# A transpose of 128 attention weights moves from one PSUM bank group to another in a two-layer hybrid attention block

## The chip, the cores and the metric

The kernel runs on one core of one Trainium2 chip. The metric is device time in microseconds: the median of three runs. One further execution was taken with the hardware profiler; all rows of the profile come from that one.

Engine names in the profile: PE is the matmul engine (PEld its weight loads), DVE the vector engine, ACT the scalar engine, POOL the general one, SP the queue that issues most DMAs. Lines (L933) are lines of the kernel's file.

## The reference

Two layers over a sequence of 512 tokens of width 1024 on float32. Each layer is a half-weighted feed-forward part with a layer norm, a token mixer with a layer norm, and a second feed-forward part with a layer norm:

```python
for l in range(DEPTH):
    x = _layer_norm(DN_ALPHA * x + 0.5 * _swiglu(x, ffn1_w1[l], ffn1_w2[l]), ln1_g[l], ln1_b[l])
    mix = _token_mix(x, w_in[l], ...)
    x = _layer_norm(DN_ALPHA * x + mix, ln2_g[l], ln2_b[l])
    x = _layer_norm(DN_ALPHA * x + 0.5 * _swiglu(x, ffn2_w1[l], ffn2_w2[l]), ln3_g[l], ln3_b[l])
```

The mixer runs three kinds of attention with eight heads of 64 each, gates their outputs and projects the sum:

- *Swa*: a window of 128 keys with a sink in the softmax.
- *Fox*: causal attention over all 512 keys, with a decay summed from forget gates.
- *Nsa*: three softmaxes for each query, each with a gate of its own: over 31 compressed keys (blocks of 32 tokens, stride 16, put through a small network), over selected blocks of 64 keys, and over a window of 512 keys. With 512 tokens there are eight blocks and eight are selected, so the second covers all of them.

The part that the change touches is the first softmax of Nsa, the weights of the compressed keys, `p_c`, on their way to `o_c = p_c @ vc`.

## The kernel before

**Stages.** Each layer is a feed-forward stage, a mixing stage and a second feed-forward stage. A float32 matrix product is made of three matmuls on high and low parts (`mm3`, L163 to L171): every weight chunk of 1024 x 128 is loaded by SP, ACT copies out its high part (`hi`, L148), and DVE subtracts to get the low part (`lo`, L149).

**The mixing stage.** The attention of two heads (index `m`) and one block of 128 queries (index `qb`) is a *unit*: an object of class Swa, Fox or Nsa with three methods. `s` makes the logits on PE (tiles sS, sF, sC, sN), then the softmax on DVE, ACT and POOL. `tr` transposes the weights on PE, 128 x 128 at a time, into PSUM tiles (ptS, ptF, ptN, ptC); `ev_pt` (L510 to L516) copies each tile back over the weights, every second one on DVE (L514) and the others on ACT (L516). `pv` multiplies values by the transposed weights into the tile po (L783, L833, L940, L946).

Units go in batches: eight of Swa, then for each `m` one batch of four (Fox and Nsa of q blocks 0 and 1) and two of two (Fox and Nsa of q block 2, then of 3). `step(cur, prev, n)` (L1115) takes one batch through `s` and the batch before it through `tr`, in slots: parts of `s`, some filler, two tiles of transposes, more filler. Filler (`pump`) is projections: chunks for later units and for the gates, each of eight parts of three matmuls (pj, L169 to L171). At the end of a step come two more filler parts, then all `pv` products of the batch in one po tile, and ACT copies that tile out, one 128 x 128 piece for each unit (L1161).

In a Nsa unit `tr` (L921) works through the two heads: for the first head one ptN tile (two, if the unit has far keys, q blocks 2 and 3), then ptC with the compressed weights of both heads, then the ptN tiles of the second head. So ptC is the second tile of a pair with ptN ahead of it (q block 0 or 1), or the first with ptN behind it.

**PSUM.** It has eight banks, shared out by tag (L77): two for `mm` (filler), three for `sc` (logits), two for `tp` (transposes and a few small tiles), one for `po`. A new tile of a tag waits until a bank of that tag is free, which is when all instructions that read the tile in it are done.

**What sets the order.** `tc.manual_schedule(engines={PE, POOL})` (L87): PE and POOL run in the order in which the code is written. PE does not overtake: if one matmul waits, all behind it wait. For ACT, DVE and SP a planner chooses the order when the program is built, from a timing that it works out itself, by the order in the code; `ev_pt` has a higher priority. Semaphores for all dependencies and for reuse of banks are put in by the framework. Each engine then runs through its own list.

Of the kernel before, what the change touches and what calls it, by code (L numbers as in the profile page):

```python
# [18 lines left out]
P = 128  # L19
# [45 lines left out]
def body(tc, a, out, depth=DEPTH):  # L65
# [15 lines left out]
    def ps(tag=None, name="ps", shape=(P, 512)):  # L81
        if tag is None:
            tag = PS_ALL[ring[0] % 8]
            ring[0] += 1
        return psp.tile(list(shape), F32, name=name, tag=tag, bufs=PS_TAGS[tag])
# [385 lines left out]
    def mix(l, wts, pend, done_ffn, xap, xa, nxt):  # L471
# [37 lines left out]
        def ev_pt(dst, src, n):  # L509

            eng[0] += 1
            with tc.high_priority(100):
                if n and eng[0] % n == 0:
                    nc.vector.tensor_copy(dst, src)  # L514
                else:
                    nc.scalar.activation(dst, src, AF.Copy)  # L516
# [118 lines left out]
        def conv(ws):  # L635
# [52 lines left out]
            def end():  # L688
                while narrow or c.n < 16:
                    feed()  # L690
                    narrow.popleft()()
                tr()
# [39 lines left out]
        class Swa:  # L732
# [37 lines left out]
            def tr(u):  # L770
                pv = u.p.rearrange("p s (b q) -> p s b q", q=P)[:, :, 0:u.nb]
                pt = ps("tp", "ptS", (P, 2, 2, P))[:, :, 0:u.nb]
                for s in range(2):
                    for b in range(u.nb):
                        nc.tensor.transpose(pt[:, s, b], pv[:, s, b], ident)
                ev_pt(pv, pt, 2)
                yield
# [59 lines left out]
        class Nsa:  # L837
# [83 lines left out]
            def tr(u):  # L921
                for s in range(2):
                    for p in u.n[s]:
                        pt = ps("tp", "ptN", (P, 2, 2, P))[:, 0:p.shape[1]]
                        for k in range(p.shape[1]):
                            for br in range(2):
                                nc.tensor.transpose(pt[:, k, br], p[:, k, br], ident)
                        ev_pt(p, pt, 2)
                        yield
                    if s == 0:  # L930
                        pc = u.pc.rearrange("p s n -> p (s n)")
                        pt = ps("tp", "ptC", (P, P))
                        nc.tensor.transpose(pt, pc, ident)  # L933
                        ev_pt(pc, pt, 2)
                        yield
# [134 lines left out]
        chunk(CKV + 4 * P, nsa_k(1))  # L1070
        chunk(CQA, set_q(m.qa, 0))
        fill.insert(len(fill) - 5, tr)
        fill.insert(len(fill) - 2, lambda: conv2(cv))
        fox_chunks(1)
# [291 lines left out]
```

## Time and profile before

| | |
|---|---|
| median of 3 runs | 2500.32 us |
| the runs | 2500.82, 2500.32, 2498.01 us |
| the profiled execution | 2500.47 us |
| its span, first to last instruction | 2498.8 us |
| granted clock of PE | 0.998 |
| instructions in the profile | 40246 |
| ptC transposes on PE (L933) | 32, in the mixing stages |
| their copies | 16 on DVE (mean 288 ns), 16 on ACT (mean 272 ns) |
| po copies on ACT (L1161) | 96 (mean 278 ns) |
| first and last ptC | at 511.9 and 1919.4 us |

How to read it: the span is covered by PE's instructions almost without a gap, and 1.7 us of the execution lie outside the span. In a timeline row stand the start, the time from the first instruction's start to the last one's end, the engine, the line, the operation, the tile written and the tiles read, the shape, how many instructions are merged, and in brackets the idle time of the engine before them with what ended it. Matmuls overlap, so the length of a row on PE is longer than the distance to the next row. In a row of waits stand who waited, for whom, the total in us, how often and the longest.

### The profile page before, as it was taken

The numbers are of one execution on the slowest core, as the hardware profiler recorded it, in microseconds if no ns is written. First come the engines' busy times: TensorE is split into PE (matmuls) and PEld (weight loads), VectorE is DVE, ScalarE is ACT, GpSimd is POOL, SyncE is SP. The second block draws the span as 40 slices with busy tenths as digits, with TensorE's granted clock in tenths as the row PEclk, the third lists the DMA queues.
The fourth block names the chain that finished last, engine by engine and source line by source line (L and its number), as shares of the span: only waits on it lengthen the run. The fifth ranks groups of instructions, "written<-read, shape, count | busy, mean of one in ns | idle before, by whom it ended". The sixth has DMA issues, their size and how long they took to land.

```text
span 2498.8 us, 40246 instructions
## 1 busy us (share of the span) xinstructions
PE 2477.1 (99%) x15547; PEld 2182.7 (87%) x15547; DVE 1655.7 (66%) x3397; ACT 1089.3 (44%) x2131; POOL 234.6 (9%) x454
## 2 busy tenths in 40 slices
PE   9999999999999999999999999999999999999998
PEld 8999887788888889998899998877888888899986
DVE  7888355587654369984479973566776534799834
ACT  4444334576642234443334443345666323344431
POOL 4000000133300000000000000002332000000000
PEclk9999999999999999999999999999999999999999
DMA  7345334633143333334323353445321534234431
GB/s 204 104 126 158 122 100 131 176 80 88 43 143 96 120 114 93 110 119 152 101 95 111 109 166 96 133 122 144 98 77 35 152 101 143 85 94 118 155 108 59
DMA packets 378095, 286.15 MB, mean 115 GB/s; under 512 B 17464, under 2 KB 349384, under 8 KB 377904
## 3 DMA queue, kind: packets, MB, share of 16 engines
q1 hardware_dynamic: 370496, 258.68, 35.5%
q0 software_dynamic: 7408, 24.90, 2.8%
q8 instruction: 122, 2.00, 0.3%
q14 instruction: 69, 0.57, 0.1%
HBM read 256.22 MB, written 17.88 MB: 110 GB/s over the span
## 4 chain that ended last, share of the span: by engine, by line
PE 95%; DVE 2%; DMA 1%; ACT 1%; issue 1%; DVEq 0%; POOLq 0%; ACTq 0%; POOL 0%; SPq 0%
PE pg L363 14%; PE acc L184 8%; PE acc L183 8%; PE acc L182 8%; PE pu L363 7%; PE pj L169 5%; PE pj L170 5%; PE pj L171 5%; PE pv L363 3%; PE gate L169 3%; PE gate L170 3%; PE gate L171 3%; PE brp L170 2%; PE brp L169 2%; PE brp L171 2%; PE sN L885 2%
## 5 line engine op out<-in xcount | busy, mean ns | idle before, releaser
L149 DVE TENSOR_TENSOR lo<-raw,hi 128x1024 fp32r<-128x1024 f32 (+2 forms) x346 | 406.0, 1180 | 484.9 <-ACT hi L148 473.2
L148 ACT ACTIVATE hi<-raw 128x1024 fp32r<-128x1024 f32 (+2 forms) x346 | 351.3, 1024 | 674.2 <-PE acc L183 230.4
L169 PE MATMUL pj<-xh,hi 128*128 128x512 f32 (+1 forms) x720 | 267.1, 371 | 0.2 <-ACT hi L148 0.2
L171 PE MATMUL pj<-xh,lo 128*128 128x512 f32 (+1 forms) x720 | 254.8, 354 | 0.0
L170 PE MATMUL pj<-xl,hi 128*128 128x512 f32 (+1 forms) x720 | 254.6, 354 | 0.0
L182 PE MATMUL acc<-hi,hs 128*128 128x512 f32 x640 | 249.7, 390 | 0.0
L184 PE MATMUL acc<-lo,hs 128*128 128x512 f32 x640 | 249.3, 389 | 0.0
L183 PE MATMUL acc<-hi,hs 128*128 128x512 f32 x640 | 249.2, 389 | 0.0
L363 PE MATMUL pg<-xh,hi 128*128 128x256 f32 x816 | 231.5, 284 | 0.9 <-ACT sn L370 0.9
L363 PE MATMUL pg<-xh,lo 128*128 128x256 f32 x816 | 231.2, 283 | 0.0
L363 PE MATMUL pg<-xl,hi 128*128 128x256 f32 x816 | 231.2, 283 | 0.0
L304 ACT ACTIVATE hi<-ws 128x1024 fp32r<-128x1024 f32 x136 | 142.4, 1056 | 131.4 <-DVE ws L296 76.0
L305 DVE TENSOR_TENSOR lo<-ws,hi 128x1024 fp32r<-128x1024 f32 x136 | 165.0, 1217 | 4.5 <-ACT hi L304 4.4
L363 PEld LDWEIGHTS pg<-xh,hi 128*128 128x128 f32 x816 | 156.8, 192 | 1.8 <-ACT sn L370 1.5
L363 PEld LDWEIGHTS pg<-xl,hi 128*128 128x128 f32 x816 | 156.8, 192 | 0.3
L363 PEld LDWEIGHTS pg<-xh,lo 128*128 128x128 f32 x816 | 156.8, 192 | 0.0
L363 PE MATMUL pu<-tl,hi 128*128 128x256 f32 x544 | 154.1, 283 | 0.0
L363 PE MATMUL pu<-th,lo 128*128 128x256 f32 x544 | 154.1, 283 | 0.0
L363 PE MATMUL pu<-th,hi 128*128 128x256 f32 x544 | 154.1, 283 | 0.0
L171 PEld LDWEIGHTS pj<-xh,lo 128*128 128x128 f32 x720 | 136.3, 189 | 19.6
L169 PEld LDWEIGHTS pj<-xh,hi 128*128 128x128 f32 x720 | 136.7, 190 | 15.4 <-issue 3.1
L170 PEld LDWEIGHTS pj<-xl,hi 128*128 128x128 f32 x720 | 136.9, 190 | 11.5 <-DVE xl L1312 0.2
(324 smaller groups left out, 5951.6 us busy)
## 6 DMA issues: line engine op xcount, KB each, us to landing
raw<-in_ffn_w_dram SPq DMA_DIRECT2D x264, 512.0 KB, 3.9
raw<-in_w_in_dram SPq DMA_DIRECT2D x56, 512.0 KB, 4.0
raw<-in_w_gate_dram SPq DMA_DIRECT2D x48, 512.0 KB, 4.1
x_sp<-xa POOLq DMA_DIRECT2D x24, 512.0 KB, 6.1
ks<-hl SPq DMA_DIRECT2D x96, 128.0 KB, 2.4
xa<-x_sp POOLq DMA_DIRECT2D x16, 512.0 KB, 5.5
raw<-in_w_out_dram SPq DMA_DIRECT2D x16, 512.0 KB, 3.4
tab<-bvec SPq DMA_DIRECT2D x16, 256.0 KB, 3.9
```

Of the source, the lines that this page charges most:

```text
L148: nc.scalar.activation(hi[:, c], raw[:, c], AF.Copy)
L149: nc.vector.tensor_tensor(lo[:, c], raw[:, c], hi[:, c].bitcast(F32), op=OP.subtract)
L169: nc.tensor.matmul(o, hi[:, k], vh, start=first, stop=False)
L170: nc.tensor.matmul(o, hi[:, k], vl, start=False, stop=False)
L171: nc.tensor.matmul(o, lo[:, k], vh, start=False, stop=last)
L182: nc.tensor.matmul(o, sh(k)[:, t], hi[:, c], start=k == 0, stop=False)
L183: nc.tensor.matmul(o, sl(k)[:, t], hi[:, c], start=False, stop=False)
L184: nc.tensor.matmul(o, sh(k)[:, t], lo[:, c], start=False, stop=k == nk - 1)
L304: nc.scalar.activation(hi, x, AF.Copy)
L305: tt(lo, x, hi.bitcast(F32), op=OP.subtract)
L363: nc.tensor.matmul(o, wx, vx, start=first and k == 0 and i == 0, stop=k == 3 and i == 2, skip_group_check=True)
L885: nc.tensor.matmul(o[:, 0:nb].rearrange("p k b j -> p (k b j)"), q, kx[:, 2 * b0:2 * (b0 + nb)].rearrange("p a b -> p (a b)"), start=i == ...
```

## The change

The tile ptC asks for a bank of the tag `po` and no longer of `tp`:

```diff
                     if s == 0:
                         pc = u.pc.rearrange("p s n -> p (s n)")
-                        pt = ps("tp", "ptC", (P, P))
+                        pt = ps("po", "ptC", (P, P))
                         nc.tensor.transpose(pt, pc, ident)
                         ev_pt(pc, pt, 2)
                         yield
```

The tag `po` has one bank. In each step it holds the tile of the value products from the first `pv` matmul to the last copy of L1161; between that copy and the next step's products it is now also taken by ptC, once in a step with q block 2 or 3, and twice, one after the other, in a step with q blocks 0 and 1. The transposes of ptN, ptF and ptS, and the small tiles, stay in `tp`. PE's order, the number of instructions and the arithmetic are the same; the planner makes ACT's, DVE's and SP's lists anew.

## Prediction

> **What bounds the kernel now.** I read first the page's busy times and its chain, then the view of waits for PE alone, then the timeline around each of those waits. On the page I look for the engine that never rests.
>
> ```profile
> PE 2477.1 (99%) x15547; PEld 2182.7 (87%) x15547; DVE 1655.7 (66%) x3397; ACT 1089.3 (44%) x2131; POOL 234.6 (9%) x454
> ...
> PE 95%; DVE 2%; DMA 1%; ACT 1%; issue 1%; DVEq 0%; POOLq 0%; ACTq 0%; POOL 0%; SPq 0%
> ```
>
> PE is busy 99% of the span and carries 95% of the chain that ends last. The kernel is PE's own instruction stream, in an order written out by hand, and the change adds or removes none of it. So only PE's pauses can be won, and only new pauses can be lost. The view of waits for PE has them all (total us, how often, longest):
>
> ```profile
> PE xT L1309 <- DMA xa<-in_x_dram: 4.6, 1, 4.6
> PE ptN L927 <- DVE pc L514: 3.0, 2, 1.5
> PE ptN L927 <- ACT p L516: 1.0, 2, 0.5
> PE ptS L775 <- ACT p L516: 0.9, 2, 0.5
> PE pg L363 <- ACT sn L370: 0.9, 2, 0.6
> PE ptC L933 <- ACT p L516: 0.5, 2, 0.2
> PE pj L169 <- ACT hi L148: 0.2, 1, 0.2
> ```
>
> L514 and L516 are the two forms of ev_pt, the copy of a transposed tile out of PSUM. Three of the rows are transposes of an Nsa unit that wait for such a copy, each twice, once in each of the two layers: 3.0 + 1.0 + 0.5 = 4.5 us. These are waits for one of the two tp banks. The row of ptS belongs to Swa steps, ahead of any ptC in the layer, and the others to stages that the change does not touch.
>
> **The three places.** The idle time in that view counts PE busy until the modelled end of its last matmul, so I take the distance from start to start instead. First number: start; second: length of the group.
>
> ```profile
> 511.25 0.38 PE L927 MATMUL ptN<-ident,p 128*128 128x128 f32 x2
> 511.85 0.30 PE L933 MATMUL ptC<-ident,pc 128*128 128x128 f32 x1 [0.23 <-ACT p L516]
> ...
> 531.21 0.27 PE L933 MATMUL ptC<-ident,pc 128*128 128x128 f32 x1
> 531.32 0.60 PE L927 MATMUL ptN<-ident,p 128*128 128x128 f32 x4
> ...
> 547.12 0.27 PE L933 MATMUL ptC<-ident,pc 128*128 128x128 f32 x1
> 547.89 0.66 PE L927 MATMUL ptN<-ident,p 128*128 128x128 f32 x4 [0.49 <-ACT p L516]
> ...
> 593.34 0.28 PE L933 MATMUL ptC<-ident,pc 128*128 128x128 f32 x1
> 595.10 0.63 PE L927 MATMUL ptN<-ident,p 128*128 128x128 f32 x4 [1.49 <-DVE pc L514]
> ```
>
> At 531.21 nothing is in the way, and the next transpose starts 0.11 us behind ptC. That is the price of one transpose on PE, and it stays, wherever its result goes. Against this measure the places cost:
> - first: two ptN and then ptC, 0.60 us where 0.22 would do: 0.38;
> - second: 547.12 to 547.89 is 0.77, less 0.11: 0.66;
> - third: 593.34 to 595.10 is 1.76, less 0.11: 1.65.
>
> Together 2.69 us in a layer, 5.38 us in both. This is the ceiling of what the change can win here.
>
> **The change part by part.** *Removed:* the 16 ptC of each layer no longer take a tp bank. In all three places ptC is either the waiter or the tile that took the bank which the waiter needed. In the first, ptC itself is held up and would find po empty. In the second and third, the first ptN of the unit had already been copied out by DVE, and ptC then took that bank:
>
> ```profile
> 545.53 0.69 DVE L514 COPY p<-ptN 128x512 f32<-128x512 f32 x1 [0.43 <-PE ptN L927]
> ...
> 592.01 0.69 DVE L514 COPY p<-ptN 128x512 f32<-128x512 f32 x1 [0.29 <-PE ptN L927]
> ```
>
> The first of these copies ends at 546.22, and without the pause the stalled ptN would start at 547.12 + 0.11 = 547.23. The second ends at 592.70, against 593.34 + 0.11 = 593.45. With ptC elsewhere the late ptN takes the bank that these copies emptied 1.0 and 0.75 us before, and has nothing to wait for. No other tile of tp fares worse: taking tiles out of a two-bank sequence puts every remaining tile's predecessor in its bank as early as before, or earlier.
>
> *Moved, at no cost:* the transpose itself and its copy. Which engine copies follows from a counter that goes on counting as before, so DVE and ACT do the same copies of the same sizes.
>
> *Added:* two waits on the single po bank. First, ptC waits until ACT has made the copies of L1161 out of the step before. Second, the step's po products wait until ev_pt has copied ptC. PE works in order, so whatever a wait costs there is paid by every filler matmul behind it. The closest case for the first wait, ACT's list and then PE's:
>
> ```profile
> 555.97 0.45 ACT L1161 ACTIVATE o<-po 128x128 f32<-128x128 f32 x2 [1.32 <-PE po L946]
> ...
> 557.51 1.06 ACT L148 ACTIVATE hi<-raw 128x1024 fp32r<-128x1024 f32 x1 [0.19 <-PE pj L170]
> ```
>
> ```profile
> 557.90 0.38 PE L927 MATMUL ptN<-ident,p 128*128 128x128 f32 x2
> 558.12 0.27 PE L933 MATMUL ptC<-ident,pc 128*128 128x128 f32 x1
> ```
>
> The copies end at 556.42 and ptC starts at 558.12: 1.70 us to spare. This is a step with q blocks 0 and 1, where ptC stands in the second pair of transposes; elsewhere ptC comes later in its step. ACT idles 1.32 us before those copies, waiting for PE: it takes them up at once. The closest case for the second wait, ACT and PE again:
>
> ```profile
> 613.61 0.27 ACT L516 ACTIVATE pc<-ptC 128x128 f32<-128x128 f32 x1
> ```
>
> ```profile
> 615.04 0.44 PE L833 MATMUL po<-p,v 128*64 128x128 f32 x4
> ```
>
> 613.88 to 615.04 leaves 1.16 us. So both new waits cost nothing as the lists of ACT and DVE now stand. No row shows a wait on po by a transpose, so I keep both ends: nothing, since both have over a microsecond to spare, up to the slower rival below. I take nothing, the value to which these rows are nearest.
>
> On these waits a page has a rule against the change. The Trainium skill, "Perfetto Trace Analysis", section Optimizing Tensor Performance, Matmuls, advises that independent matmul groups rotate through different PSUM banks, so that copying one out overlaps the next group; one bank for ptC and the products gives that up. By that rule ptC and the copies of L1161 run one behind the other; by the rows they do so already, 1.70 us apart, and the sum stays. The Trainium skill, "PSUM — Partial Sum Buffer", section PSUM bank collisions raise a hardware error, adds that two engines must keep off one bank even at different columns, so ptC would have to wait for the last of the copies and not only for those it overwrites; 1.70 us is counted from the last one, and the sum stays again.
>
> **What is late next.** PE coming earlier does not make DVE and ACT earlier where these are full. Next come the products of the same step, which read the last transposed tile. ACT and PE, second place; then PE and DVE, third place:
>
> ```profile
> 551.49 0.51 ACT L900 ACTIVATE p<-p,stN 128x256 f32<-128x256 f32 x1 [1.25 <-DVE stN L725]
> ...
> 553.10 0.57 ACT L516 ACTIVATE p<-ptN 128x512 f32<-128x512 f32 x1
> ```
>
> ```profile
> 553.98 1.26 PE L946 MATMUL po<-p,v 128*64 128x128 f32 x20
> ...
> 601.13 1.92 PE L946 MATMUL po<-p,v 128*64 128x128 f32 x32
> ```
>
> ```profile
> 599.15 0.69 DVE L514 COPY p<-ptN 128x512 f32<-128x512 f32 x1
> ...
> 604.20 0.29 DVE L514 COPY p<-ptF 128x128 f32<-128x128 f32 x1 [2.91 <-PE ptF L826]
> ```
>
> - Second place. L946 is the line of the products. By then PE is 0.38 + 0.66 = 1.04 us ahead, and L946 would start at 552.94. The copy that it reads ends at 553.67, and stands behind an ACT that waited for DVE; DVE's timeline has no idle entry between 545.53 and that point, and its start at 545.53 waits for a ptN that only the first place has brought forward, by 0.38. So the copy ends at 553.29, and L946 waits 0.35. Kept so far: 0.69.
> - Third place. PE is 0.69 + 1.65 = 2.34 ahead at 601.13, which makes 598.79. DVE waited for a ptN at 592.01, and its timeline has no idle entry from there to the end of its copy at 599.84, and 0.69 earlier that is 599.15. L946 waits until then: 0.36 lost. Kept: 1.98 us.
> - After that DVE stood idle for 2.91 us, waiting for PE, so it has room to follow, and nothing more is given back.
>
> The sum: 1.98 us in a layer, 3.96 in both. The profiled execution, 2500.47 us, becomes 2496.5; the median of the runs, 2500.32, stands 0.15 us below that execution and becomes **2496.4 us**. As a difference of 0.16% it is less than the 0.2% (5.0 us) which a measurement of this kernel can about tell from no change.
>
> **The rivals.**
> - *Nothing is given back.* ACT's and DVE's orders are not written out: the planner sets them from its own timing of PE's order and the bank waits, and with the wait gone it may put the copies of the last ptN earlier. ACT had 1.25 us of idle time just before 551.49. Then 5.4 us are kept or, with a pause elsewhere gone too, somewhat more: 2494.9. For it speaks that idle time, against it that DVE is full in the third place, whatever the order.
> - *Nothing is won.* The banks were not what PE waited for, or the planner's new order puts other copies late by as much as is won. The named releasers speak against the first: all are copies out of tp. For the second speaks that the order decides by tenths of a microsecond in three places already. Time: 2498 to 2503, say 2500.
> - *Slower: the po wait takes over.* Place: the three steps of each layer with q blocks 0 and 1, after the first in a layer. If the planner puts weight splits (L148, 1.06 us each) ahead of the L1161 copies on ACT, ptC waits and all PE's filler behind it. It decides from the second split on, since 2.12 exceeds 1.70; with three it costs 3.18 - 1.70 = 1.48 us at each of six places, 8.9 in all: 2496.4 + 8.9 = 2505.3. Against it: ACT now reaches the copies idle, with nothing ahead of them.
>
> The rule on rotating banks, in the Trainium skill's "Perfetto Trace Analysis" as above, is this last rival; the trace so far bears out the distance of 1.70 us and no wait.
>
> **How the numbers follow.** My forecast (1.9 to 5 us won) has 0.42; nothing given back, 0.26; nothing won, 0.20; slower by the po wait, 0.12. Faster by over 0.2% is the second case, 0.26; within 0.2% the first and third, 0.62; slower 0.12. The range runs from 2493.5, the ceiling of 5.4 and 1.4 for the scatter of the runs (2498.01 to 2500.82), to 2503, the upper end of the third case; the dear end of the po wait stays outside.
>
> **What would show it.** In the waits of PE after the change, the rows of ptN and ptC behind L514 and L516 are gone. If the give-back is real, po L946 appears there behind ACT and DVE copies, each 0.3 to 0.4 us. Right in the second rival: these rows stay, or new ones of sN, sC or pj stand beside them. Right in the third: ptC waits for ACT o L1161. If PE's waits in the two mixing stages sum to more than now, the prediction is wrong, and the order of ACT's and DVE's lists is the first place to look. A change in the feed-forward stages would be one for which I have no cause.

## The result

| | before | after |
|---|---|---|
| median of 14 runs each | 2500.47 us | 2494.04 us |
| lowest and highest | 2498.01, 2502.91 | 2492.38, 2498.15 |
| the profiled execution | 2500.47 us | 2494.47 us |
| its span | 2498.8 us | 2492.8 us |
| granted clock of PE | 0.998 | 0.998 |

The ratio of the times is 0.9976, with a 95% interval of 0.9968 to 0.9983: faster by 0.24%, 4.3 to 8.0 us. The two profiled executions differ by 6.0 us. This lies a little beyond what the prediction called the ceiling (5.4 us, which the interval still holds), and beyond its forecast (3.96 us, just outside the interval).

The page of the kernel after, busy times and chain, as they were shown of before:

```profile
PE 2476.4 (99%) x15547; PEld 2182.5 (88%) x15547; DVE 1656.1 (66%) x3397; ACT 1089.0 (44%) x2131; POOL 225.1 (9%) x454
...
PE 98%; DVE 1%; DMA 0%; ACT 0%; issue 0%; DVEq 0%; POOLq 0%; SPq 0%; POOL 0%; ACTq 0%
```

PE has as many matmuls as before and as much busy time, in a shorter span. Its share of the chain rose from 95% to 98%. Most of this rise is not the change's: between 50 and 250 us, ahead of the first mixing stage, some 75 us of the chain ran over other engines before and next to none after. The waits of PE after (the whole view: who waited, for whom, total us, how often, longest):

```profile
PE xT L1309 <- DMA xa<-in_x_dram: 4.6, 1, 4.6
PE ptS L775 <- ACT p L516: 0.9, 2, 0.5
```

The rows of ptN and ptC are gone, and no row of po has come. The rows of pg and pj have gone too, in stretches where every engine's order is the same in both kernels, so this is not the change's doing. The two profiles differ there for a reason that stays open: the kernel after left the program's start 1.5 us behind (last section), and PE of the kernel before lost 1.65 us up to 240 us, most of it at pg at 140.6 and 223.2 us. From there on, up to the first mixing stage, the two kernels are within 0.2 us of each other.

The three places in the timeline of PE after (start, length, as before):

```profile
511.16 0.38 PE L927 MATMUL ptN<-ident,p 128*128 128x128 f32 x2
511.38 0.27 PE L933 MATMUL ptC<-ident,pc 128*128 128x128 f32 x1
...
546.60 0.27 PE L933 MATMUL ptC<-ident,pc 128*128 128x128 f32 x1
546.70 0.60 PE L927 MATMUL ptN<-ident,p 128*128 128x128 f32 x4
...
592.08 0.27 PE L933 MATMUL ptC<-ident,pc 128*128 128x128 f32 x1
592.19 0.60 PE L927 MATMUL ptN<-ident,p 128*128 128x128 f32 x4
```

From start to start it is now 0.22, 0.10 and 0.11 us, the price of transposes with nothing in the way; it was 0.60, 0.77 and 1.76. PE's order is the same in both kernels, so each of its 15547 matmuls can be set against its twin. The lead of the kernel after grows at the three places by 0.389, 0.656 and 1.654 us, together 2.70, and in the mixing stages no step takes more than 0.1 us of it back. Over the mixing stage of the first layer it grows by 2.95 us, over that of the second by 2.92, together 5.87. The 0.25 that the three places do not explain come in small steps. The largest is a fourth place of the same kind; here are PE's rows of before, then of after:

```profile
640.84 0.27 PE L933 MATMUL ptC<-ident,pc 128*128 128x128 f32 x1
641.02 0.63 PE L927 MATMUL ptN<-ident,p 128*128 128x128 f32 x4
```

```profile
637.92 0.27 PE L933 MATMUL ptC<-ident,pc 128*128 128x128 f32 x1
638.03 0.60 PE L927 MATMUL ptN<-ident,p 128*128 128x128 f32 x4
```

Before, ptN stood 0.18 us behind ptC, 0.07 more than undisturbed, and another 0.03 was lost inside the ptN group. No idle time is shown there: ptC's modelled end (641.11) lies beyond ptN's start.

**Why nothing was given back.** In the second place the prediction had the last ptN's copy on ACT end late. ACT's rows of after, then PE's:

```profile
550.89 0.57 ACT L516 ACTIVATE p<-ptN 128x512 f32<-128x512 f32 x1
...
552.55 0.31 ACT L867 ACTIVATE pc<-pc,stN 128x32 f32<-128x32 f32 x1
```

```profile
552.74 1.92 PE L946 MATMUL po<-p,v 128*64 128x128 f32 x32
```

The copy ends at 551.46, 1.28 us ahead of the products. In ACT's list of before, both exponentials of L867 stood ahead of this copy; in the new list they come after it and after two more of L900. The second of them and the copy, in the kernel before:

```profile
552.79 0.30 ACT L867 ACTIVATE pc<-pc,stN 128x32 f32<-128x32 f32 x1
...
553.10 0.57 ACT L516 ACTIVATE p<-ptN 128x512 f32<-128x512 f32 x1
```

In the third place the copy is on DVE:

```profile
597.31 0.69 DVE L514 COPY p<-ptN 128x512 f32<-128x512 f32 x1
598.03 0.90 DVE L730 TENSOR_SCALAR p<-p,stN,gt 128x128 f32<-128x128 f32 x2
...
601.27 0.29 DVE L514 COPY p<-ptF 128x128 f32<-128x128 f32 x1 [1.43 <-PE ptF L826]
```

```profile
598.21 1.92 PE L946 MATMUL po<-p,v 128*64 128x128 f32 x32
```

It ends at 598.00, 0.21 us ahead of L946. The two L730 that now follow it stood ahead of it in the list of before:

```profile
596.13 0.61 DVE L730 TENSOR_SCALAR p<-p,stN,gt 128x128 f32<-128x128 f32 x2
...
599.15 0.69 DVE L514 COPY p<-ptN 128x512 f32<-128x512 f32 x1
```

DVE is as full as it was; what changed is which of its work comes first. In the two traces PE, POOL and SP run in the same order; ACT's order differs at 52 of its 2131 positions and DVE's at 106 of 3397, all of them in the mixing stages, between 514 and 1837 us of the kernel before.

**The new waits on po.** The closest case of each in the first layer, ACT's rows of after and then PE's:

```profile
554.73 0.45 ACT L1161 ACTIVATE o<-po 128x128 f32<-128x128 f32 x2 [1.47 <-PE po L946]
...
610.68 0.26 ACT L516 ACTIVATE pc<-ptC 128x128 f32<-128x128 f32 x1
```

```profile
556.88 0.27 PE L933 MATMUL ptC<-ident,pc 128*128 128x128 f32 x1
...
612.12 0.44 PE L833 MATMUL po<-p,v 128*64 128x128 f32 x4
```

From the end of the copies of L1161 (555.18) to ptC are 1.70 us, as predicted; from the end of ptC's copy (610.94) to the products 1.18, against 1.16. In the second layer the same two distances are 1.70 and 1.14 us.

### The profile page after: what moved, and what is told of

Its sections match the earlier page's. It is cut to its first block, busy times and chain, and to the rows that moved or that the text cites. A ratio compares the mean times of both kernels' runs of the same rounds, so it can differ in the third digit from the quotient of the medians.

```text
span 2492.8 us, 40236 instructions
## 1 busy us (share of the span) xinstructions
PE 2476.4 (99%) x15547; PEld 2182.5 (88%) x15547; DVE 1656.1 (66%) x3397; ACT 1089.0 (44%) x2131; POOL 225.1 (9%) x454
## 4 chain that ended last, share of the span: by engine, by line
PE 98%; DVE 1%; DMA 0%; ACT 0%; issue 0%; DVEq 0%; POOLq 0%; SPq 0%; POOL 0%; ACTq 0%
PE pg L363 16%; PE pu L363 8%; PE acc L184 8%; PE acc L182 8%; PE acc L183 8%; PE pj L169 5%; PE pj L170 5%; PE pj L171 5%; PE pv L363 4%; PE gate L169 3%; PE gate L170 3%; PE gate L171 3%; PE brp L171 2%; PE brp L170 2%; PE brp L169 2%; PE sN L885 2%
## 5 line engine op out<-in xcount | busy, mean ns | idle before, releaser
L148 ACT ACTIVATE hi<-raw 128x1024 fp32r<-128x1024 f32 (+2 forms) x346 | 351.3, 1024 | 677.7 <-PE acc L183 230.3
L169 PE MATMUL pj<-xh,hi 128*128 128x512 f32 (+1 forms) x720 | 267.0, 371 | 0.1
L169 PEld LDWEIGHTS pj<-xh,hi 128*128 128x128 f32 x720 | 136.7, 190 | 15.3 <-issue 3.1
```

The source lines that it names most:

```text
L148: nc.scalar.activation(hi[:, c], raw[:, c], AF.Copy)
L169: nc.tensor.matmul(o, hi[:, k], vh, start=first, stop=False)
```

## The experiments

All kernels start from the kernel after, and each ratio is against the kernel before. **Theory A** explains the result so: a transpose waits no more once its tile has a bank that is idle at that moment, and the gain is kept because the planner put the late copies ahead of other work. **Theory B** is the rival, and each expectation says what it means for its run.

**late_copy: the last ptN copy goes back to its old place.** In q block 3 it is held behind the exponentials of L867 on ACT (m = 0) and behind two L730 on DVE (m = 1), as in the lists of before; a second line of the same form keeps two exponentials of L900 in their order, and otherwise the lists are those of the kernel after. `m.pce` and `m.n0` name the exponential and the L730 that it waits behind. The edit's core:

```diff
-                        ev_pt(p, pt, 2)
+                        with tc.issue_after((m.pce, m.n0)[u.m].ins) if u.qb == 3 and s and p is u.n[1][1] and u.m < 2 else tc.high_priority(100): ev_pt(p, pt, 2)
```

> The changed kernel with four copies held back, two in each layer: in the second place (the step before the products of m = 0, q block 3) ACT makes the last ptN copy behind the two exps of L867, as in the kernel before; in the third place (m = 1) DVE makes it behind two norms of L730, as before. Nothing else in any engine's order differs from the changed kernel. Theory A (the lead on PE was kept because the planner's new order puts these copies earlier): po L946 waits in all four places, 0.3 to 0.5 us each, 1.4 to 1.8 us in all; the span goes from 2492.8 to 2494.2 to 2494.6. Theory B (the copies would have been early enough in the old order too, the reckoning of the give-back was wrong in itself): no wait at L946, span 2492.6 to 2493.0.

Median 2496.4 us (11 runs), ratio 0.9987 (0.9978 to 0.9996). ACT and PE at the second place, then DVE and PE at the third:

```profile
550.64 0.31 ACT L867 ACTIVATE pc<-pc,stN 128x32 f32<-128x32 f32 x1
...
550.95 0.57 ACT L516 ACTIVATE p<-ptN 128x512 f32<-128x512 f32 x1
```

```profile
551.05 2.48 PE L946 MATMUL po<-p,v 128*64 128x128 f32 x32
```

```profile
596.21 0.60 DVE L730 TENSOR_SCALAR p<-p,stN,gt 128x128 f32<-128x128 f32 x2
596.84 0.69 DVE L514 COPY p<-ptN 128x512 f32<-128x512 f32 x1
```

```profile
597.11 2.44 PE L946 MATMUL po<-p,v 128*64 128x128 f32 x32
```

Now the copies end 0.47 and 0.42 us after the products' first matmul, and the row of 32 matmuls takes 2.48 and 2.44 us, where it takes 1.92 in the kernel after. Against that kernel's matmuls, PE falls back at L946 by 0.57 and 0.52 us in the first layer and by 0.57 and 0.53 in the second: 2.19 us, more than the 1.4 to 1.8 of theory A. This is the give-back of the prediction, at its two places, and it is there only when the copies stand behind that work as before. The span of the profile, 2493.2 us, fits neither theory's range; this execution left the program's start 1.5 us ahead of the kernel after's (last section), so the two spans cannot be set against each other. The median moves the same way, 2.4 us up, but the intervals of the two ratios overlap; it is the matmuls' starts that decide. PE's view of waits has no row of L946 in this kernel (its only rows are those of xT and ptS, as after): counted from the modelled end of the matmul ahead, 551.43, PE idles 0.14 us before the late matmul at 551.57, too little to show. These waits show only from start to start.

**again: the kernel after, unchanged,** run beside n2_po, c_first and kv_sc below.

> The changed kernel once more, beside the next three on the same chip. Both theories: the same as before, 2492.5 to 2496 us, ratio to the kernel before 0.997 to 0.998; PE's waits hold xT and ptS only.

2493.84 us (9 runs), ratio 0.9976 (0.9967 to 0.9986): the result repeats. PE's waits hold one row that was not expected, pj L169 behind ACT's L148, 0.5 us at the start of the program (8.4 us).

**q3_only: only q block 3's ptC goes to po.**

```diff
-                        pt = ps("po", "ptC", (P, P))
+                        pt = ps("po" if u.qb == 3 else "tp", "ptC", (P, P))
```

> Only the ptC of q block 3 go to po, 8 of 32; the others stay in tp. Theory A (the gain is the sum of single places): the second and third place and the small one at 641 us are gone (0.71, 1.68 and 0.10 us in a layer by the shifts), the first stays (0.42): the span is 0.8 us over the changed kernel's, 2493.6, and PE's waits show ptC behind L516 0.5 us in 2 cases. Theory B (the gain is spread over the step, through the planner's order): the span lies between 2494 and 2498.

One run, 2493.86 us. The wait of the first place is back in PE's waits, and those of the second and third (ptN) stay away:

```profile
PE ptS L775 <- ACT p L516: 0.9, 2, 0.5
PE ptC L933 <- ACT p L516: 0.5, 2, 0.2
```

Against the kernel after, PE falls back by 0.39 us at the first place and by as much at its twin in the second layer, and nowhere else in the mixing stages by more than 0.15 us (at hid, L657, the network of the compressed keys). So the gain is a sum of single places, and ptC of q block 3 alone earns the second and third place. The one run's time says nothing on 0.7 us, nor does its span of 2492.2 us, below both theories': this execution too left the program's start 1.5 us ahead.

**sc_bank: ptC in a bank of the logits (sc) and not in po.** If any bank outside tp would do, this should be as fast.

```diff
-                        pt = ps("po", "ptC", (P, P))
+                        pt = ps("sc", "ptC", (P, P))
```

> The changed kernel with ptC in one of the three sc banks, those of the logits, and not in po. Theory A (what counts is a bank that is idle when ptC comes; po is, the sc banks are not, they turn over with every unit): the waits of ptN behind L514 and L516 are gone as well, but ptC, sF or sN wait for logits and copies in their place; span 2494 to 2500. Theory B (anything out of tp serves): span 2492.5 to 2493.1, and no new row among PE's waits.

2501.16 us (10 runs), ratio 1.0006 (0.9997 to 1.0015): all of the gain is lost. From PE's waits:

```profile
PE ptC L933 <- DVE stN L725: 2.8, 6, 0.6
PE sN L885 <- DVE stF L725: 1.4, 2, 0.7
...
PE sN L885 <- ACT pc L516: 0.9, 2, 0.5
```

The waits of ptN are gone here too, but ptC now waits until DVE has read logits (L725), and logits wait for other logits or until ptC is copied out. It is po's idle time that pays, not the relief of tp alone.

**n2_po: the ptN tiles of the second head go to po as well,** so that ptC and they take turns in one bank.

```diff
-                        pt = ps("tp", "ptN", (P, 2, 2, P))[:, 0:p.shape[1]]
+                        pt = ps("po" if s else "tp", "ptN", (P, 2, 2, P))[:, 0:p.shape[1]]
```

> The changed kernel, and the ptN tiles of the second head go to po too, so that ptC and the ptN behind it take the one bank in turn. Theory A (one bank without rotation makes each transpose wait for the copy of the one before): from the distances of the ptC and their copies in the kernel before, 0.5 to 2.4 us each for twelve pairs in a layer, 11 us, 23 in both, less what later waits absorb; 2508 to 2520 us, with ptN behind L514 and L516 as the largest rows of PE's waits. Theory B (a wait on po is covered by what is queued elsewhere): under 2498.

2527.3 us (4 runs), ratio 1.0109 (1.0095 to 1.0122): slower, and by more than was expected. From PE's waits:

```profile
PE ptN L927 <- ACT pc L516: 13.9, 12, 2.4
PE ptN L927 <- DVE pc L514: 6.7, 12, 1.5
```

At 24 of the 32 ptC, where ptN comes directly behind, it now waits for ptC's copy; at the other eight, filler stands between them. Here the rule of the Trainium skill, "Perfetto Trace Analysis", section Optimizing Tensor Performance, Matmuls, that independent groups should rotate through different banks, holds: 20.6 us of waits at 24 places. From start to start the loss in the mixing stages is 35.9 us: about 27.7 at ptN, 1.8 at the products of Fox and 6.2 in stretches where the clock is halved, which the last section shows. The spans differ by 32.3 us, since this profile's start, without the half clock, was 3.2 us ahead.

**c_first: all ptC at the start of the step,** right behind the copies of L1161, with po as their bank.

```diff
+            for u in prev:
+                if u.br == 0: u.trc()
             it, iu = chain(u.tr() for u in prev), chain(u.s() for u in cur)
```

Here `trc` holds the four lines of ptC, which `tr` no longer has.

> The changed kernel with the ptC transposes of a step moved ahead of everything else in the step, directly behind the products of the step before; the alternation of the copies between ACT and DVE shifts with them. This is the po wait of my slower rival, with the distance of 1.70 us taken away. Theory A (only that distance hides the wait): PE waits for the copies of L1161, about 1.0 us in each of twelve steps of a layer, and the second ptC of four steps for the copy of the first, 0.6 us; 14 us in a layer, 2515 to 2535 us, ptC behind ACT o L1161 in PE's waits. Theory B (PE's queue or other slack covers it): under 2500.

2527.08 us (4 runs), ratio 1.0112 (1.0098 to 1.0126). The time is in the expected range by luck: from PE's waits less than a third of the loss is the one that was meant (its lines are three further down: L936 is ptC, L1164 the copies of po):

```profile
PE ptC L936 <- POOL pc L730: 13.8, 9, 2.7
PE ptC L936 <- ACT o L1164: 7.5, 10, 1.0
...
PE ptC L936 <- POOL p L730: 2.1, 4, 0.6
```

The bank costs 7.5 us at 10 places, up to 1.0 us each, once its distance of 1.70 us is taken away. More, 13.8 us, is that the weights are not ready so early: POOL still scales them. So the run shows that the wait on po exists, and does not show that it alone would cost 33 us.

**kv_po and kv_sc: the row of ptS.** The transposes ptS wait 0.9 us in the two layers together, in `tp`, for the bank which the small tile kv has taken. kv goes to po in the one and to sc in the other:

```diff
-            p = ps("tp", "kv", (P, 3, 64))
+            p = ps("po", "kv", (P, 3, 64))
```

> The changed kernel, and the small tile kv (conv2) goes from a tp bank to po as well. Theory A (a transpose waits on PE because a longer-lived tile holds one of the two tp banks; po is free between the copies of one step and the products of the next): the last wait of a transpose, ptS behind L516, 0.64 us from start to start in each layer, is gone; 1.3 us less, span 2491.5. Theory B (the second bank is not what ptS waits for, or kv keeps po so long that the products wait): the row stays, or po L783 appears among the waits of PE; span 2492.8 or more.

> The changed kernel, and kv goes to a bank of sc. Until the first Fox step those three banks serve one unit at a time, and kv is read out 3.3 us before the next logits come. Theory A (a bank that is idle at that moment is what counts): ptS no longer waits, 0.67 us in a layer, and no products wait for vbd either; the span is 1.3 us below that of the changed kernel beside it, no row but xT among PE's waits. Theory B (the time that ptS saves is waited for again a step later, whichever bank kv is in, since vbd comes late): no difference to the changed kernel.

kv_po: 2493.0 us (10 runs), ratio 0.9975 (0.9965 to 0.9984). The row of ptS is gone, and in PE's waits and timeline stands another:

```profile
PE po L783 <- ACT vbd L713: 1.2, 2, 0.6
```

```profile
494.23 0.88 PE L783 MATMUL po<-p,v 128*64 128x128 f32 x12 [0.60 <-ACT vbd L713]
```

In each layer PE gains 0.70 us at ptS, and loses 0.67 at the next products: the bank is held until ACT has copied kv in L713, and that copy waits for POOL. That the span, 2491.3 us, is near theory A's is chance, since this execution left the program's start 1.5 us ahead of the kernel after's; by the rows theory B is right. kv_sc: 2493.1 us (9 runs), ratio 0.9973 (0.9963 to 0.9983). Its whole view of PE's waits:

```profile
PE xT L1309 <- DMA xa<-in_x_dram: 4.5, 1, 4.5
PE pj L169 <- ACT hi L148: 0.2, 1, 0.2
```

Nothing takes the place of the wait: against again, PE gains 0.70 us at ptS in each layer and keeps them. The medians differ by 0.7 us, less than their intervals. By the matmuls kv_sc is the best version of all, 1.4 us ahead of the unchanged kernel beside it; by the times alone the two cannot be told apart.

Not tried: ptC in a bank of `mm`.

## Why the prediction was right in part and wrong in part

The time fell within the range, near its lower end, which is the case in which nothing is given back. The forecast of 2496.4 us did not come true; the first rival, "nothing is given back" (2494.9 us, chance 0.26), did.

- *PE bounds the kernel, only its pauses can be won.* Right: the same matmuls in the same order, and the gain is the sum of their pauses.
- *The three places.* Right in place and size: 0.38, 0.66 and 1.65 worked out, 0.389, 0.656 and 1.654 measured. q3_only brings the first of them back alone.
- *The ceiling of 5.38 us.* Too low by about 0.5 (5.87 measured): steps of up to 0.07 us, as at 641.02, lie below what the view of waits shows, so it does not hold all of PE's waits, against what the prediction said. Taken from start to start for every ptN and ptC, they could have been found.
- *The added waits on po cost nothing.* Right: 1.70 and 1.18 us to spare after, and no row of po in the waits. That "any bank" is not the reason shows in sc_bank.
- *What is late next: 0.35 and 0.36 us given back in each layer.* **This is the step that failed.** The mechanism is real: in late_copy it takes back 0.52 to 0.57 us at each place. But it needs these copies in their old order on ACT and DVE, and in the kernel after the order is a new one. The forecast held the lists fixed, against the kernel's description, which says that the planner makes them anew. "DVE is full in the third place, whatever the order" was true of DVE's sum of work and wrong as a reason: the products need one copy of that work, and it moved ahead of two L730. At the second place it moved ahead of two L867.
- *The sign by which it was to be checked,* "po L946 appears there ... each 0.3 to 0.4 us", was no good sign: late_copy has 2.2 us of such waits and no row.
- *A change in the feed-forward stages would be one without a cause.* The rows of pg are such a change; they differ between the two profiled executions and not between the kernels' orders. Taken with the program's start, they leave 0.1 us between the two kernels at the first mixing stage.
- *Slower, the po wait takes over.* Did not happen, since nothing was put ahead of the copies of L1161. c_first shows that the wait begins when the distance goes.

What stays open: how the planner came to its new order. That it put the copies earlier because its own timing no longer has the bank wait fits the lists, but was only argued.

## What to carry to other kernels

A tile that lives for a microsecond is best put into a bank that is idle at that moment, whatever kind of tile the bank was meant for; look up first from which last reader to which next writer the bank really is free (po here 1.70 and 1.18 us around ptC; kv's last reader came too late for po). Where a planner makes the lists, taking a wait away changes them: before booking that a gain is given back by a late copy, ask whether that copy could stand earlier, and read only its place, not the engine's load. Measure pauses of PE from start to start against an undisturbed twin, since the view of waits leaves out those that a matmul's modelled end covers, wholly or nearly.

## What the runs showed of the hardware

A long pause of PE can cost more than itself, since the granted clock may halve after it. In n2_po ptN starts 2.06 us behind ptC, at 546.87. The stretches around it (stretch, then busy time of each engine, the granted clock PEclk, DMA share and GB/s):

```profile
545.00:547.00 2.00, 0.21 (x2) 0.14 (x2) 1.97 (x11) 1.94 (x7) 0.00 (x0) 1.00 0.00 0
547.00:548.50 1.50, 1.50 (x10) 1.34 (x11) 1.44 (x4) 0.92 (x4) 0.41 (x1) 0.99 0.34 85
548.50:550.00 1.50, 1.50 (x5) 1.17 (x4) 1.50 (x7) 0.00 (x0) 1.50 (x5) 0.50 0.88 265
550.00:551.50 1.50, 1.50 (x6) 1.11 (x5) 1.36 (x12) 1.30 (x6) 0.44 (x2) 0.50 0.00 0
551.50:553.00 1.50, 1.50 (x9) 1.32 (x8) 0.00 (x0) 1.22 (x6) 0.00 (x0) 0.87 0.00 0
```

The clock is 0.50 for 3.41 us, from 1.6 us after the pause (548.49), and the matmuls there follow each other at 0.43 us and not at 0.23. After its twin in the second layer, also 2.06 us, the clock stays at full; after pauses of 2.63 us it fell both times. The pause of 1.76 us which the change removed was not followed by it in either layer of before, so this is no part of the gain; but one of 1.83 us in c_first was, and its twin of 1.82 was not.

The traces' records of the clock show what decides. In the midst of a run (46 to 2470 us) a half clock lasts 3.41 us or twice that, and such stretches lie on one grid: in n2_po they start at 548.49, 647.47 and 1900.16, which is 29 and 396 steps of 3.41 us apart. Taking these steps as windows, the window ahead of the half clock and that of the twin pause are:

```profile
545.07:548.48 3.41, 1.62 (x11) 1.48 (x11) 3.32 (x14) 2.79 (x9) 0.39 (x1) 1.00 0.14 35
1797.76:1801.17 3.41, 1.72 (x11) 1.56 (x12) 3.32 (x13) 2.68 (x9) 0.50 (x2) 1.00 0.20 50
```

PE (the first busy time) is busy for 1.62 us of the one and 1.72 of the other. Ahead of the other half clocks that follow a pause it is 1.46 and 1.05 us in n2_po, 1.44, 0.98 and 0.71 in c_first; in none of the ten runs does a half clock begin after a window of this grid with 1.72 us or more (1.92 at the pause of 1.76 us in before). So in these runs the clock fell after a window in which PE was busy less than about half of the time, and a pause of 2 us does that or not by where it lies on the grid.

The Trainium skill, "TensorE: Matmul & The Clock Gate", section What's actually happening, tells of a half-rate clock after an idle window of about 3.4 us that runs freely. The grid of 3.41 us agrees with the free running; that pauses of 1.8 to 2.6 us were enough, in windows with PE busy for up to 1.62 us, does not agree with a window that has to be idle throughout. A half clock also stands at the start of every profile but n2_po's, between 36.9 and 44.9 us, for 3.41 us in some and 6.83 in others (before 3.41, after 6.83). This moves a span by 1.5 us, which is why spans of single profiles are not compared here to the microsecond.
